# A list scheduler's model of its transfers: a later landing and a lower rate

## The chip, the cores and the metric

One core of one Trainium2 chip runs the kernel alone. The metric is device time in microseconds (us) for one execution. Engines are named as the profile names them: PE (matrix products; PEld loads its weights), DVE (vector), ACT (scalar), POOL (GpSimd) and SP (SyncE, which only issues DMAs here).

## The reference, cut to what matters

Two layers of a decoder trunk run for a prompt of 1024 tokens and for 8 samples of 4 tokens; both share the weights. Width is 1024, everything is float32.

```
layer 0:  h = rmsnorm(x);  proj = h @ w_in_a              # 3 groups x 4 heads x (q, k, v), and 4 cross queries
          mix = dilated sliding-window attention, 3 groups combined per head
                (prompt: banded softmax; samples: caches of 128, 512 and 2048 rows)
layer 1:  h = rmsnorm(x);  proj = h @ w_in_b
          mix = S5 state space (32 groups x 64 complex states), gelu, gated by w_glu
both:     cross = 4-head attention into 256 memory tokens (k, v = rmsnorm(mem) @ w_mem_kv)
          x = x + [mix | cross] @ w_out
          f = silu(a) * b  with  a, b = causal conv3(rmsnorm(x) @ w_up);   x = x + f @ w_down
outputs:  y of both, the updated caches, memory k/v, S5 states and conv states
```

## The kernel before

All 1056 tokens (1024 and 32) stand along the free dimension, in three column groups of 352, and 128 features on the partitions. A float32 product is made of three matmuls on a high and a low half (`mm3`); a weight tile is loaded by SP (`wload`, usually 512 KB), its high half is cast by ACT (`whigh`) and its low half is the difference, made by DVE or POOL (`wlow`). A pool of 20 buffers "B" holds raw and split weights and most activations.

The order of all instructions is written out when the program is built, by a list scheduler in the kernel itself. The dense products form a main stream; everything else (attention, sample attention, cross attention, S5, loading and turning inputs) consists of generators in 14 `Lane`s. After each `mm3` the main stream calls `pump`, which steps a lane when its gate is open. The gate (`gate`, `due`, `ready`) compares a clock that the scheduler keeps, `Meter`, with the time at which the operands of the lane's next step will be there by that clock. `Meter.note` books each instruction: a duration from the operation and size for the four computing engines, and for a DMA the issue, then a landing on a serial queue per issuing engine. `wtick` uses the same clock to decide when `whigh` and `wlow` are put out. Where nothing is left for the main stream, `until` calls `pump(True)`, which steps the lane with the earliest gate even if it isn't open. The engines then run their programs in order, with semaphores for the data: an instruction put out before its data is there blocks what is behind it on its engine.

`Meter` doesn't model the wait of a DMA for a free buffer. A step that is placed by its position in a loop, as the weight splits and reloads inside `up_tiles` and `hid_group` (the FFN), doesn't ask the clock.

Steps that the text below names: `x_turn`, `x_squares`, `x_norm` and `x_scale` load the input rows in nine tiles, transpose them on PE, take sums of squares on ACT, and make the normed halves in A tiles; `mem_kv` is the main stream beside them. `attn`, `scores` and `combine_head` are the prompt's attention, with partial results through DRAM (`og`, `xm`). `swa` is the samples' attention on DVE, with the caches in two 1 MB ring tiles in pool L, one fetched ahead, in lane 2, which `pump` serves last. `cross_s` is the samples' cross attention, whose memory rows POOL loads. In layer 1 `s5_u_evac` writes u to DRAM (`d_u`), reads it back in eight slices and appends `s5_states`, whose first step waits for them; `s5_out` uses `d_t` and `d_cl`.

Every operation passes through the wrapper at L216, so all rows have that line and are told apart by tile names.

Of the kernel before, what the change touches and what calls it, by code (L numbers as in the profile page):

```python
# [111 lines left out]
class Meter:  # L112
# [51 lines left out]
    def note(self, eng, op, args, kw):  # L164
        outs = [kw[k] for k in ("out", "accum_out") if kw.get(k) is not None] or [args[0]]
        ins = list(args["out" not in kw:]) + [v for k, v in kw.items() if k not in ("out", "accum_out")]
        ins = [a for a in ins if hasattr(a, "tensor")]
        out = outs[0]
        n = out.free_size()
        src = next((a for a in ins if a.free_size() >= n), out)  # L170
        start = max(self.t[eng], self.ready(ins, eng), *(self.used.get(o.tensor.name, 0.0) if o.space == bass.MemoryType.PSUM else 0.0 for o in outs))
        if op == "dma_start":
            if out.space != bass.MemoryType.DRAM:
                start = max(start, self.t["tensor"] - 4.0)
            self.t[eng] = start + (1.0 if eng == "gpsimd" else 0.05)
            self.dma[eng] = max(self.dma.get(eng, 0.0), self.t[eng] + 1.6) + n * out.ap[0][1] * 4 / 350e3
            end = self.dma[eng] + 0.2
        else:
            if eng == "tensor":
                wide = ins[0].dtype == F32  # L180
                turn = op == "transpose"
                cost = 0.107 if turn else max(n * 4 / 2400 + 0.008, 0.107) + 0.03 if wide else max(n / 2400, 0.025) + 0.0025
            elif eng == "scalar":
                vecs = sum(hasattr(kw.get(x), "tensor") for x in ("scale", "bias", "accum_out"))
                cost = (0.051 if src.space == bass.MemoryType.PSUM else 0.094) + n * 0.833e-3 + 0.0935 * vecs
            elif eng == "gpsimd":
                cost = 0.147 + n * 2.105e-3
            else:
                k = max(n, src.free_size()) if op.startswith("reduce") else n
                vecs = any(hasattr(kw.get(x), "tensor") for x in ("scalar", "scalar1", "scalar2"))  # L190
                fast = op == "tensor_scalar" and all(a.space != bass.MemoryType.PSUM for a in ins + outs)
                cost = 0.065 + 0.065 * vecs + k * 1.04e-3 * (6 if op == "reciprocal" else 0.5 if fast else 1)
            end = self.t[eng] = start + cost
        for o in outs:
            lo, hi = self.span(o)
            w = self.written.setdefault(o.tensor.name, [])
            w[:] = [x for x in w if not (lo <= x[0] and x[1] <= hi)] + [(lo, hi, end, eng if op != "dma_start" else "dma")]
        for a in ins + outs:
            self.used[a.tensor.name] = max(self.used.get(a.tensor.name, 0.0), end)
# [2409 lines left out]
```

## Time and profile before

| | us |
|---|---|
| median of 3 runs (2932.32 to 2938.57) | 2933.89 |
| the profiled execution | 2938.67 |
| its span, first to last instruction | 2936.7 |
| PE busy | 2735.2 (93%) |
| PEld busy | 2612.5 (89%) |
| DVE busy | 2070.4 (71%) |
| ACT busy | 1216.3 (41%) |
| POOL busy | 560.1 (19%) |

The mean granted PE clock is 0.972 of full speed. The DMA queues moved 431.56 MB, 147 GB/s over the span. PE is the engine that is nearly always busy, so a change of the time has to be a change of PE's idle time or of its clock; the other engines' idle time matters only where PE waits behind it.

### The profile page before, as it was taken

What the parts mean: (1) busy time and instruction counts of PE and PEld (TensorE: products, weight loads), DVE (VectorE), ACT (ScalarE), POOL (GpSimd) and SP (SyncE); (2) the same over time, 40 slices, a digit from 0 to 9 for tenths busy, and PEclk for the clock granted to TensorE, in tenths of its full rate; (3) what the DMA queues carried; (4) which work ended last, traced back from release to release, by engine and by line L of the source; (5) the groups of instructions that cost most, each with busy time, mean ns of one, the idle gap of its engine ahead of it and who ended that gap; (6) DMA issues with size and microseconds to landing.
All of it is one profiled execution on the core that took longest, in us unless ns stands there. A gap on an engine that the chain in (4) does not pass through costs nothing.

```text
span 2936.7 us, 50915 instructions
## 1 busy us (share of the span) xinstructions
PE 2735.2 (93%) x18896; PEld 2612.5 (89%) x18896; DVE 2070.4 (71%) x5937; ACT 1216.3 (41%) x3045; POOL 560.1 (19%) x551
## 2 busy tenths in 40 slices
PE   6999889999979999999998997888999999999999
PEld 5899778999969989999998887777998999999998
DVE  7477776787895777878859876645468787886434
ACT  6455554454542544444421123245344444443211
POOL 3221222322334400000022344011250000001220
PEclk8999999999989999999999998999999999999999
DMA  7234765666583423333482524843443234336421
GB/s 246 82 86 129 210 192 175 171 185 195 172 226 129 155 87 116 123 116 123 143 270 83 186 84 163 242 132 99 166 147 123 95 123 131 109 131 230 148 95 60
DMA packets 378883, 431.56 MB, mean 147 GB/s; under 512 B 31190, under 2 KB 333300, under 8 KB 377212
## 3 DMA queue, kind: packets, MB, share of 16 engines
q1 hardware_dynamic: 335516, 364.23, 38.9%
q0 software_dynamic: 20048, 47.95, 5.7%
q10 hardware_dynamic: 23072, 16.14, 2.0%
q8 instruction: 149, 2.44, 0.3%
q14 instruction: 98, 0.80, 0.1%
HBM read 345.10 MB, written 172.37 MB: 176 GB/s over the span
## 4 chain that ended last, share of the span: by engine, by line
PE 43%; DVE 37%; ACT 11%; issue 4%; DMA 4%; ACTq 1%; POOL 1%; SPq 0%; DVEq 0%; POOLq 0%
PE pd L216 34%; DVE B L216 21%; PE pm L216 9%; ACT B L216 7%; DVE S L216 6%; DVE T L216 3%; DVE L L216 3%; DVE M L216 3%; ACT S L216 2%; DMA L<-in_cache_win_kv 1%; ACT M L216 1%; ACT A L216 1%; DVE A L216 1%; ACTq L216 1%; ACT L L216 1%
## 5 line engine op out<-in xcount | busy, mean ns | idle before, releaser
L216 PE MATMUL pd<-A,B 128*128 128x352 f32 (+2 forms) x10992 | 1790.4, 317 | 44.1 <-DVE B L216 32.6
L216 PEld LDWEIGHTS pd<-A,B 128*128 128x128 f32 x10992 | 1645.9, 190 | 74.7 <-issue 39.4
L216 ACT CAST B<-B 128x512 fp32r<-128x512 f32 (+4 forms) x430 | 313.8, 751 | 618.1 <-DVE B L216 320.9
L216 POOL TENSOR_TENSOR B<-B,B 128x1024 fp32r<-128x1024 f32 (+3 forms) x95 | 236.9, 2494 | 1703.7 <-ACT B L216 1410.8
L216 DVE TENSOR_TENSOR B<-B,B 128x512 fp32r<-128x512 f32 (+5 forms) x517 | 409.5, 800 | 212.5 <-ACT B L216 205.6
L216 PE MATMUL pd<-L,B 128*128 128x264 f32 (+1 forms) x2976 | 449.7, 303 | 18.6 <-DVE L L216 9.5
L216 PEld LDWEIGHTS pd<-L,B 128*128 128x128 f32 x2976 | 417.0, 190 | 22.6 <-DVE L L216 10.2
L216 DVE TENSOR_TENSOR B<-pd,B 128x352 f32<-128x352 f32 x408 | 202.4, 518 | 222.0 <-PE pd L216 221.0
L216 ACT COPY B<-pm 128x512 f32<-128x512 f32 (+5 forms) x261 | 129.9, 507 | 211.2 <-PE pm L216 198.5
L216 PE MATMUL pd<-B,B 128*128 128x264 f32 (+2 forms) x1308 | 201.9, 303 | 2.5 <-POOL B L216 2.0
L216 DVE SCALAR_TENSOR_TENSOR B<-B,S,B 128x1023 f32<-128x1023 f32 (+1 forms) x152 | 198.3, 1305 | 0.0
L216 PE MATMUL pm<-const,B 128*128 128x128 f32 (+6 forms) x1103 | 161.4, 276 | 35.6 <-DVE B L216 7.8
L216 PEld LDWEIGHTS pd<-B,B 128*128 128x128 f32 x1308 | 179.6, 188 | 6.7 <-POOL B L216 2.6
L216 PEld LDWEIGHTS pm<-const,B 128*128 128x128 f32 (+4 forms) x1103 | 130.0, 148 | 56.9 <-issue 17.4
L216 ACT COPY S<-pm 128x256 f32<-128x256 f32 (+5 forms) x281 | 89.6, 346 | 166.2 <-PE pm L216 157.5
L216 ACT CAST A<-B 128x352 fp32r<-128x352 f32 (+3 forms) x148 | 97.5, 669 | 141.3 <-DVE B L216 49.9
L216 ACT COPY B<-pd 128x352 f32<-128x352 f32 (+4 forms) x211 | 103.6, 540 | 98.9 <-PE pd L216 90.3
L216 PE MATMUL pm<-const,S 128*128 128x128 f32 (+3 forms) x468 | 86.5, 292 | 45.5 <-DVE S L216 23.3
L216 DVE SCALAR_TENSOR_TENSOR L<-L,T,L 128x128 f32<-128x128 f32 x404 | 121.0, 375 | 3.7 <-DMA L<-in_cache_win_kv 3.6
L216 ACT ACTIVATE B<-B 128x352 f32<-128x352 f32 (+3 forms) x127 | 94.6, 750 | 68.7 <-DVE B L216 64.9
L216 PEld LDWEIGHTS pm<-const,S 128*128 128x128 f32 (+2 forms) x468 | 60.3, 159 | 65.0 <-ACT S L216 24.8
L216 DVE TENSOR_TENSOR A<-B,A 128x1056 fp32r<-128x1056 f32 (+3 forms) x78 | 92.5, 1193 | 11.8 <-ACT A L216 11.5
(210 smaller groups left out, 2628.9 us busy)
## 6 DMA issues: line engine op xcount, KB each, us to landing
B<-in_w_up SPq DMA_DIRECT2D x88, 512.0 KB
hd<-B SPq DMA_DIRECT2D x44, 528.0 KB
B<-hd SPq DMA_DIRECT2D x44, 528.0 KB
B<-in_w_down SPq DMA_DIRECT2D x44, 512.0 KB
B<-in_w_in_a SPq DMA_DIRECT2D x40, 512.0 KB
B<-xsp SPq DMA_DIRECT2D x32, 528.0 KB
L<-in_cache_win_kv SPq DMA_DIRECT2D x16, 1024.0 KB
L<-in_cache_win_kv SPq DMA_DIRECT2D x64, 256.0 KB
```

Source lines behind the costliest of these rows:

```text
L216: return f(*args, **kw)
```

## The change

In the booking of a DMA, the time between its issue and the earliest begin of its bytes goes from 1.6 to 2.2 us, and the rate of the queue from 350 to 250 bytes a nanosecond. No instruction, size or buffer is changed by itself; the order in which the generators are interleaved may change wherever a gate hangs on a DMA.

```diff
             self.t[eng] = start + (1.0 if eng == "gpsimd" else 0.05)
-            self.dma[eng] = max(self.dma.get(eng, 0.0), self.t[eng] + 1.6) + n * out.ap[0][1] * 4 / 350e3
+            self.dma[eng] = max(self.dma.get(eng, 0.0), self.t[eng] + 2.2) + n * out.ap[0][1] * 4 / 250e3
             end = self.dma[eng] + 0.2
```

Here `n * out.ap[0][1] * 4` is the size in bytes, `start` the time at which the issuing engine is free and the source is written, and `end` the landing that `ready` returns (0.2 us more is added for another engine's use of it).

## Rows read from the trace of the kernel before

**Rows 1.** Busy time by stretch: length, PE, PEld, DVE, ACT, POOL, granted clock, DMA.

```profile
0.00:80.00 80.00, 55.86 (x285) 46.86 (x285) 60.41 (x139) 48.61 (x93) 30.24 (x29) 0.87 0.74 244
80.00:800.00 720.00, 667.84 (x4438) 631.93 (x4439) 519.75 (x2532) 371.15 (x1212) 177.90 (x197) 0.97 0.55 157
800.00:900.00 100.00, 82.47 (x447) 73.15 (x446) 88.50 (x330) 41.78 (x114) 33.83 (x29) 0.90 0.78 227
...
1040.00:1470.00 430.00, 413.41 (x3302) 409.02 (x3301) 347.14 (x613) 195.09 (x443) 4.67 (x2) 0.99 0.38 123
1470.00:1690.00 220.00, 205.55 (x1279) 197.15 (x1278) 173.21 (x562) 43.81 (x61) 61.37 (x54) 0.98 0.53 177
1690.00:2060.00 370.00, 319.62 (x2098) 283.10 (x2099) 224.72 (x564) 146.12 (x369) 86.28 (x106) 0.94 0.48 144
...
2660.00:2937.00 277.00, 269.13 (x1711) 266.49 (x1709) 122.83 (x191) 56.74 (x72) 45.42 (x18) 0.99 0.38 133
```

**Rows 2.** Waits of PE over the span: us in total, times, longest us.

```profile
PE pd L216 <- DVE B L216: 43.2, 51, 5.4
PE pm L216 <- ACT S L216: 32.5, 30, 4.7
PE pm L216 <- DVE S L216: 23.3, 17, 9.2
...
PE pm L216 <- DMA B<-in_g_mix: 7.3, 1, 7.3
...
PE pm L216 <- DMA L<-d_u: 4.7, 2, 3.0
...
PE pm L216 <- DMA B<-d_cl: 0.9, 1, 0.9
```

**Rows 3.** Waits of DVE and ACT for DMAs, the same columns.

```profile
ACT A L216 <- DMA B<-hd: 39.8, 8, 17.7
ACT B L216 <- DMA B<-in_w_down: 38.8, 8, 9.7
...
DVE T L216 <- DMA B<-og: 11.5, 5, 5.5
...
DVE M L216 <- DMA L<-scr: 4.2, 2, 2.7
...
DVE L L216 <- DMA L<-in_cache_win_kv: 3.6, 2, 2.5
...
DVE M L216 <- DMA L<-in_cache_win_kv: 3.2, 3, 2.8
```

**Rows 4.** DMA issues of POOL: count, KB each, median us from issue to landing.

```profile
L<-scr POOLq DMA_DIRECT2D x36, 256.0 KB, 4.6
...
B<-in_cache_mem_kv POOLq DMA_DIRECT2D x16, 512.0 KB, 6.1
...
A<-in_cache_mem_kv POOLq DMA_DIRECT2D x16, 512.0 KB, 4.3
...
d_t<-M POOLq DMA_DIRECT2D x1, 2048.0 KB, 12.9
...
d_win<-S POOLq DMA_DIRECT2D x16, 128.0 KB, 2.0
```

**Rows 5.** Timeline of SP around the first read of d_u: start, length, what.

```profile
1824.45 0.63 SPq L216 DMA_DIRECT2D d_u<-B  x1
...
1829.01 5.36 SPq L216 DMA_DIRECT2D L<-d_u  x8
```

**Rows 6.** Timeline of PE there, with the idle time before a row.

```profile
1836.75 0.69 PE L216 MATMUL pm<-L,B 128*64 128x136 f32 x8 [3.01 <-DMA L<-d_u]
...
1886.94 0.69 PE L216 MATMUL pm<-L,B 128*64 128x136 f32 x8 [1.74 <-DMA L<-d_u]
```

**Rows 7.** Timeline of PE in the first stretch.

```profile
34.25 0.49 PE L216 MATMUL pm<-const,B 96*128 96x96 f32 x4
...
46.88 1.60 PE L216 MATMUL pd<-M,const 128*128 128x128 f32 x6 [2.75 <-DVE M L216]
49.64 1.59 PE L216 MATMUL pd<-M,const 128*128 128x128 f32 x6 [1.16 <-DVE M L216]
...
63.20 0.66 PE L216 MATMUL pd<-A,B 128*128 128x352 f32 x1 [9.18 <-ACT A L216]
```

**Rows 8.** Timeline of ACT in the first stretch: the last row's sum of squares.

```profile
43.06 1.06 ACT L216 ACTIVATE B<-B 96x1024 f32<-96x1024 f32 x1
```

**Rows 9.** Groups of DVE in 800:900: count, busy us, mean ns.

```profile
L216 DVE SCALAR_TENSOR_TENSOR L<-L,T,L 128x128 f32<-128x128 f32 x68 | 18.7, 347 | 0.0
```

## The prediction, made before the change was run

> **What bounds the kernel now.** The busy table by stretch comes first [rows 1]. PE is busy in nearly all of each stretch; what is left over is PE's idle time: 24.1 us in 0:80 (80 less 55.86), 52.2 in 80:800, 17.5 in 800:900, 16.6 in 1040:1470, 14.5 in 1470:1690, 50.4 in 1690:2060, 7.9 in 2660:2937. The whole span has 201.5 us of it (2936.7 less 2735.2). An edit that adds no work and removes none can move the time only inside these 201.5 us, and through the clock where PE pauses (0.87 in 0:80, 0.90 in 800:900). The second view is the waits of PE [rows 2]: most of them are for DVE and ACT results; only 12.9 us are direct waits for a DMA (7.3 + 4.7 + 0.9), and the 7.3 is the first transfer of all, which no order changes. The third is the waits of DVE and ACT for DMAs [rows 3]: these say where a consumer was put out before its data had landed, which is what the edited lines are about. The fourth is how long a transfer really takes [rows 4], as far as the trace has it (POOL's issues; for SP's there is no landing column, so SP's are read from a wait that a landing ended).
>
> **The change part by part.** It removes and adds no instruction. It moves consumers of DMAs later in the order, by what the booked landing grows: 0.6 us a transfer, and bytes/250 less bytes/350 a nanosecond. For 512 KB (524,288 bytes) that is 1.50 us of bytes before and 2.10 after. Booked from issue to landing: SP 0.05 + 1.6 + 1.50 + 0.2 = 3.35 before, 4.55 after; POOL, with 1.0 for the issue, 4.30 and 5.50. The trace has 4.3 and 6.1 us for POOL's 512 KB, 4.6 for 256 KB (booked 3.55, then 4.45), 12.9 for 2 MB (8.8, then 11.8) and 2.0 for 128 KB (3.2, then 3.9) [rows 4]. So the new booking is nearer for large and crowded transfers and further off for small ones.
>
> The Trainium skill (DMA: Bandwidth & Descriptors, section Anatomy of one DMA — SWDGE (gpsimd) path) gives about 2.0 us plus bytes at 436 GB/s for a DMA of this path. By that page 512 KB would estimate at 3.2 us, the old booking would be late enough already, and the change would only delay; the trace's 6.1 and 4.6 disagree with it, its 2.0 for 128 KB agrees.
>
> *Beginning, 0:80.* No engine waited for an input tile: the only wait for a DMA there is that for g_mix [rows 2], so later bookings can only hold consumers back. The queue carries 2 memory tiles, 9 input tiles and 8 weight tiles before the last input tile is due: some 19 times 0.6 us of bytes, 11.4 us; the clock of the main stream itself starts about 2 us later, because its first operands are booked later too, and three of the tiles are smaller. I take the last tile's turn as 6.5 us later against the main stream. In the trace that turn is at 34.25 [rows 7], but ACT takes its sum of squares only at 43.06 [rows 8], 8 us after the turn ended: ACT is behind, and this backlog hides the delay as long as ACT has other work. What is late next is the chain that PE already waits for: 2.75 + 1.16 + 9.18 us for the normed input [rows 7]. Bounds: nothing (all in ACT's backlog) and +7 (none of it). I take the middle, +3.5, because ACT's other work there, the weight casts, can't all move forward.
>
> *S5's read-back, 1690:2060.* The first slice chain is booked as: write of 512 KB and 64 KB, two tables of 512 KB, eight reads of 72 KB, all serial: before, 1.65 + 1.50 + 0.19 + 3.00 + 8 x 0.21 + 0.2 = 8.2 us; after, 2.25 + 2.10 + 0.26 + 4.19 + 8 x 0.29 + 0.2 = 11.4 us. In the trace the write is issued at 1824.45 [rows 5] and PE is released by the last read at 1836.75 [rows 6], 12.3 us. The 3.2 us later booking therefore covers the 3.01 us that PE stood, and the 1.74 us of the second such place; dense matmuls of the main stream take their place, and the lane's data come no later than before. Bounds: -5.6 (4.7 + 0.9, all direct waits but the first) and 0 (a lane step blocked a little later by something else). I take -4.5, nearest to the row.
>
> *Combining the heads, mostly 80:800.* DVE stood 11.5 us in 5 waits for og [rows 3]. Three loads of 260 KB in a row are booked 1.65 + 3 x 0.76 + 0.2 = 4.1, after it 2.25 + 3 x 1.07 + 0.2 = 5.7: up to 1.5 us of each wait goes, 7.5 us of DVE time. DVE is busy 519.75 of 720 us there [rows 1], so most of it was no loss to PE. Bounds -7.5 and 0; taken -2.
>
> *Samples' cross attention, 1690:2060.* Its ring loads landed in 4.3 us and were booked at 4.30; they will be booked at 5.50, 1.2 us too late. Two lanes take four rounds of two loads: 4 x 2 x 1.2 = 9.6 us at most, but the next round is fetched while one is worked on, which hides it; without that cover the lanes end up to 5 us later, in a stretch where PE is idle for 50.4 us anyway. Bounds 0 and +5; taken +1.
>
> *FFN, 1040:1470, 2265:2660 and the down projections.* ACT's largest waits for DMAs are here, 39.8 and 38.8 us [rows 3]. But the loads and splits stand at fixed places, and PE is busy 269.13 of 277 us with them in 2660:2937 [rows 1]. Taken 0, bounds -2 and +2.
>
> *Everything else.* Each gate that opens later lets another lane go first, and that shifts all that follows in 80:900 and 1690:2060. Of the 120.1 us of PE idle time there (52.2 + 17.5 + 50.4) a tenth either way is 12 us. I take 0, and keep both ends.
>
> Sum: +3.5 - 4.5 - 2 + 1 = -2.0 us. The profiled execution took 2938.67, 1.97 more than its span and 4.78 more than the median of the runs shown. 2938.67 - 2.0 = 2936.7 for such an execution; in terms of the median, 2933.89 - 2.0 = 2932 us.
>
> **The rivals.** *The sample attention falls behind (slower).* A ring tile of `swa` comes as one 1 MB load or four of 256 KB; four are booked 0.05 + 1.6 + 4 x 0.75 + 0.2 = 4.8 us before, 6.6 after. One is fetched ahead, and one tile's work is 16 operations of 347 ns [rows 9], 5.6 us: before, the booked landing was just inside the work that covers it, after it is just outside. Then each tile waits some 1 us by the scheduler's clock, the lane that is served last loses its turn, and its last tiles are pushed to 800:900, where DVE is already busy 88.5 of 100 us. Two tiles late cost 11 to 12 us of DVE there, which PE waits for: -2 + 12 = +10, 2944 us. It decides from the point where the lane enters 800:900 with two tiles more than now. For it: the chain there is DVE's. Against: DVE's own bookings, not the landings, may set the lane's pace, since DVE waited for these tiles only 3.6 + 3.2 us.
>
> *Stalls go everywhere (faster).* If an order with truer landings spares PE an eighth of its waits for ACT S, DVE S and DVE B (32.5 + 23.3 + 43.2 = 99 us) [rows 2], that is 12 us more: -14, 2920 us. For it: blocks on DVE and ACT are what PE waits for. Against: only 23 us of DVE's waits are for DMAs at all.
>
> *Nothing hangs on it.* Gates set by engines and free PSUM banks instead of landings leave the order as it is: 2934 us. Against it: og and d_u were early by the rows.
>
> *Landings were right already.* If 512 KB mostly lands about when it was booked before, as in POOL's 4.3 us for the cross attention's ring [rows 4], the late bookings hold back the beginning and the cross attention, +3.5 + 1, and spare nothing: 2938 us. Against it: 6.1 us for the same size in the other ring, and the 12.3 us of the read-back. The page of the Trainium skill named above, DMA: Bandwidth & Descriptors, speaks for it.
>
> **How the numbers follow.** Forecast 0.40, with its own range 2924 to 2940; sample attention late 0.22; stalls go 0.24; nothing 0.07; landings right 0.07. About 0.2% (5.9 us, below 2928 or above 2940) is what a measurement of this kernel can tell. Faster: 0.23 of the faster rival and 0.08 of the forecast, 0.31. Slower: 0.21 of the slower rival and 0.05 of the forecast and of the last, 0.26. Same: 0.43. The range goes from a little under the faster rival, 2917, to some way over the slower one, 2949.
>
> **What would show it.** Right: the waits of PE for d_u and d_cl are gone, those of DVE for og are near 4 us, PE's idle time in 0:80 is 3 to 4 us more, and the FFN stretches keep their lengths within 2 us. Wrong: 0:80 is no longer or is 8 us longer; the d_u waits stay; 800:900's work takes 10 us more with DVE full (sample attention); or the difference stands in 80:800, spread over many waits for ACT and DVE, which no term of the sum has.

## The result, and the profile after

The changed kernel takes 2966.38 us (median of 4 runs, 2964.05 to 2973.09), the kernel before 2936.23 in the runs beside it: a ratio of 1.0110, 95% interval 1.0090 to 1.0129. It is slower by 30 us, outside the predicted range. The page of the profiled execution (2973.09 us) has the busy times, and the granted clock in 40 slices:

```profile
span 2971.2 us, 50957 instructions
...
PE 2753.0 (93%) x18896; PEld 2622.7 (88%) x18896; DVE 2072.2 (70%) x5940; ACT 1217.5 (41%) x3045; POOL 547.5 (18%) x548
...
PEclk8999999999989999999999998989999999999999
```

PE has the same 18,896 instructions as before. In this pair of profiles it is busy 17.8 us longer for them (2753.0 less 2735.2) and idle 16.7 us longer (218.2 less 201.5), and the mean granted clock is 0.967 in place of 0.972: for the same products a lower clock shows as a longer busy time. How large this part of the loss is can't be read from one pair. The profiled execution is the longest of the four and has the lowest clock (the other three: 0.968, 0.970 and 0.971), and the profile of `st_rest` below is 18.9 us longer than before with PE busy only 3.6 us longer. The waits of PE over the span, against [rows 2]:

```profile
PE pd L216 <- DVE B L216: 54.5, 63, 3.3
PE pm L216 <- ACT S L216: 46.9, 28, 13.0
PE pm L216 <- DVE S L216: 19.9, 16, 9.0
...
PE pm L216 <- DMA B<-in_g_mix: 7.2, 1, 7.2
```

The waits for d_u and d_cl [rows 2] are gone, as predicted. The waits for ACT S grew from 32.5 to 46.9 us, the longest from 4.7 to 13.0, and DVE B (the low halves of weights are written there) from 51 waits to 63. Against [rows 3], DVE and ACT:

```profile
ACT A L216 <- DMA B<-hd: 38.3, 10, 12.5
ACT B L216 <- DMA B<-in_w_down: 31.4, 6, 13.1
...
ACT L L216 <- DMA d_y<-L: 23.7, 2, 18.9
```

```profile
DVE T L216 <- DMA B<-og: 1.8, 1, 1.8
```

DVE's wait for og fell from 11.5 to 1.8 us. ACT's longest stand for `d_y<-L`, which is a store of its own, grew from 10.7 us, once, to 18.9. The kernel before has this row for it:

```profile
ACT L L216 <- DMA d_y<-L: 10.7, 1, 10.7
```

Against [rows 4], this page also has landings of SP's DMAs (count, KB each, median us from issue to landing):

```profile
B<-in_w_up SPq DMA_DIRECT2D x88, 512.0 KB, 5.2
...
B<-in_w_down SPq DMA_DIRECT2D x44, 512.0 KB, 4.6
...
L<-in_cache_win_kv SPq DMA_DIRECT2D x64, 256.0 KB, 5.3
```

The 512 KB weight tiles of the feed-forward blocks land on SP after 4.6 to 5.2 us, where 3.35 was booked before and 4.55 now. So for these the new numbers are nearer, and the kernel is slower with them. No one pair of numbers fits all: SP's other 512 KB transfers have medians from 2.6 us (`out_y_prompt`) to 10.9 (`B<-d_win`) on the same page.

To see where, the dense matmuls of the main stream are counted. There are 15,360 of them, in the same order in every kernel here, so a block of time is what lies between two of them. How much longer each block is than before, in us, from one profile each (the blocks are named by the times of before; the last column is the whole span):

```
                    0-68  68-969  969-1457  1457-1729  1729-2093  2093-2666  2666-2928 |  span
changed             +3.8   +11.2      +0.0       +8.9       +6.4       +0.8       +3.3 | +34.4
lat_only            +2.0    +0.4      +0.6       +4.6       -6.2       +4.1       -0.3 |  +5.3
rate_only           +1.1    -4.9      +1.0       +5.6       +4.3       +1.5       +3.4 | +12.1
earlier             +5.1    +7.7      -0.4       -1.6      +17.6       +1.4       -0.3 | +30.1
tiny                +3.4    +2.5      +0.1       -0.7       -0.2       +1.9       -0.0 |  +7.0
st_begin            +3.6    +0.7      -0.2       +0.0       +1.9       -0.0       +0.0 |  +6.1
st_att              +2.0   +11.3      +0.0       +1.0       +4.1       +2.6       +0.0 | +21.0
st_rest             +2.4    -6.0      -0.2       +8.8       +9.9       +0.9       +3.1 | +18.9
after_dy_pool       +3.7    +8.0      +1.3       +7.9       -8.7       -0.0       +3.3 | +16.0
before_dy_pool      +1.1    -3.3      -0.2       +0.5       -4.6       +0.1       -0.2 |  -6.1
s5_new_dy_pool      +0.2    -3.4      -0.0       +0.8      -12.4       +0.8       +0.3 | -13.6
s5_new_dy_pool_gate +0.2    -0.1      +0.2       +1.2       -9.4       +1.4       -0.1 |  -6.2
swa_old             +3.8    +6.6      +0.8       +5.2       -2.9       +1.8       +3.2 | +18.4
swa_new             +4.0    +0.1      -0.0       +2.9       +2.2       +0.0       -0.1 |  +9.2
ffn0_new            +4.7    -1.3      -0.4      +12.0       +0.7       -0.2       -0.3 | +15.3
st_att_gate         +2.0   +21.9      +1.5       +2.2       +1.2       -2.9       +0.0 | +25.9
before_gate         +1.8    +4.6      -0.4       -0.5       +2.6       -0.2       -0.1 |  +7.9
```

How far one profile can be trusted is read from four kernels whose booking is that of before up to 969 (st_rest, before_dy_pool, s5_new_dy_pool, ffn0_new): 0-68 comes out +0.2 to +4.7 there, 68-969 -6.0 to -1.3. The +3.8 of the beginning is therefore no finding; the +11.2, and the +8.9 and +3.3 further on (within 3 and 0.3 us of before wherever the booking there was the old one), are. In 1729-2093, kernels with the old booking and the old S5 stores come out +0.7 to +4.1 (st_begin, st_att, swa_new, ffn0_new, st_att_gate, before_gate), so the changed kernel's +6.4 alone would say little; what S5 costs is read from the tests on it below.

### The profile page after: what moved, and what is told of

Same layout as the page of the kernel before. It is cut to its first block, busy times and chain, and to the rows that moved or that the text cites. A ratio compares the mean times of both kernels' runs of the same rounds, so it can differ in the third digit from the quotient of the medians.

```text
span 2971.2 us, 50957 instructions
## 1 busy us (share of the span) xinstructions
PE 2753.0 (93%) x18896; PEld 2622.7 (88%) x18896; DVE 2072.2 (70%) x5940; ACT 1217.5 (41%) x3045; POOL 547.5 (18%) x548
## 5 line engine op out<-in xcount | busy, mean ns | idle before, releaser
L216 DVE TENSOR_TENSOR B<-B,B 128x512 fp32r<-128x512 f32 (+5 forms) x524 | 417.1, 805 | 218.4 <-ACT B L216 210.3
L216 POOL TENSOR_TENSOR B<-B,B 128x1024 fp32r<-128x1024 f32 (+3 forms) x88 | 218.0, 2479 | 1726.7 <-ACT B L216 1479.8
L216 PE MATMUL pd<-B,B 128*128 128x264 f32 (+4 forms) x1322 | 211.0, 307 | 13.5 <-DVE B L216 10.6
L216 ACT COPY B<-pm 128x512 f32<-128x512 f32 (+3 forms) x260 | 129.8, 511 | 214.9 <-PE pm L216 206.8
L216 PE MATMUL pm<-const,B 128*128 128x128 f32 (+5 forms) x1111 | 162.0, 276 | 34.9 <-issue 14.6
L216 ACT COPY S<-pm 128x256 f32<-128x256 f32 (+4 forms) x278 | 89.0, 347 | 175.5 <-PE pm L216 167.4
L216 DVE CUSTOM_DVE_ANT_0 M<-L,L 128x128 f32<-128x128 f32 x384 | 94.9, 311 | 13.7 <-PE pm L216 3.8
```

Source lines behind the costliest of these rows:

```text
L216: return f(*args, **kw)
```

## The experiments

Times are medians; each ratio is against the kernel before, run beside it.

**Which of the two numbers, and which direction.** Four versions of the booked line: only the later landing (2.2 us, 350), only the lower rate (1.6 us, 250), the opposite of the change, and a tiny change.

```diff
-self.t[eng] + 1.6) + n * out.ap[0][1] * 4 / 350e3    # before
+self.t[eng] + 1.0) + n * out.ap[0][1] * 4 / 583e3    # earlier
+self.t[eng] + 1.65) + n * out.ap[0][1] * 4 / 345e3   # tiny
```

lat_only: 

> Only the begin of the bytes is booked later (2.2 us), the rate stays 350. Theory 1 (later bookings hold lanes back, in proportion): between before and after, about +12 to +20 us of the +30. Theory 2 (any other order of the lanes costs, whatever the booking says): some +10 to +35 us, no relation to the size of the edit. Rival (only the sample attention's 1 MB tiles matter, by their bytes): within 8 us of before.

rate_only: 

> Only the rate is booked lower (250), the begin stays at 1.6 us. Theory 1: +10 to +20 us. Theory 2: +10 to +35 us with its losses in other places than those of the full change. Rival (sample attention by its bytes): nearly the whole +30, with 18 us of it between 725 and 985.

earlier: 

> The opposite edit of the same size: begin 1.0 us, 583 bytes a nanosecond. Theory 1: no slower than before, the first 80 us some 0 to 4 us shorter, the read-back of d_u stands longer (+2 to +5). Theory 2: slower by 10 us or more, too, though the edit has the other sign.

tiny: 

> A very small edit of the same sign: 1.65 us and 345 bytes a nanosecond; a 512 KB transfer is booked 0.07 us later. Theory 1: within 3 us of before. Theory 2: it moves the time by several us in either direction, as its order differs in all queues.

Measured: lat_only 2943.81, ratio 1.0010 (0.9995 to 1.0024); rate_only 2950.62, 1.0029 (1.0017 to 1.0040); earlier 2969.16, 1.0096 (1.0071 to 1.0122); tiny 2945.67, 1.0015 (0.9997 to 1.0034). The halves come to 0.4% and the whole to 1.1%, so they don't add up, and both halves lie below what either theory had expected of them. Booking *earlier* costs as much as booking later, so a theory that later bookings cost in proportion to how much later they are is out. But it costs in another way. In `earlier` PE itself waits for transfers:

```profile
PE pm L216 <- DMA L<-d_u: 13.1, 2, 7.1
PE pm L216 <- DMA B<-in_state_s: 11.7, 1, 11.7
```

Both waits lie in its longest block, 1729-2093 (+17.6). The kernel before waits 4.7 us for d_u [rows 2] and never for `in_state_s` (a little ahead of that place it stands 9.2 us for DVE S, which `earlier` doesn't, so not all of the 11.7 is new); the changed kernel waits for neither. So consumers put out too soon cost here what the booking is meant to prevent, and the loss of the changed kernel is of another kind.

**Which part of the program.** The new numbers hold only in one part (`self.lat, self.rate` in the booked line, set in `run`): up to the first `mem_kv`, from there to the end of the first output projection, or from the first feed-forward block on.

```diff
         kmt, kv = self.mem_kv(0)
+        self.m.lat, self.m.rate = 2.2, 250e3      # st_att: from here ...
...
+        self.m.lat, self.m.rate = 1.6, 350e3      # ... to here
         self.bulk_on = True
         self.drain(0)
         self.ffn(0, self.s5_prep())
```

st_begin: 

> The new booking holds only up to the end of the first layer's memory keys and values (the first 70 us or so); behind that the old one. Theory A, the stages add up: the time is 3 to 4 us above the kernel before (the beginning was 3.8 us longer in the changed kernel's trace), and the stretches from 68 us on keep their lengths within 2 us each. Theory B, what comes behind depends on every start: the beginning is 3 to 4 us longer and some later stretch differs by more than 5 us in either direction.

st_att: 

> The new booking holds only from the attention on to the end of the first layer's output projection (about 70 to 1040 us). Theory A, the stages add up: 729 to 969 us is about 18 us longer as in the changed kernel, 438 to 729 some 10 us shorter, the whole 8 to 14 us above before, and 1040 us onward keeps its lengths. Theory B: the attention comes out otherwise, since its lanes start at another place of the main stream than in the changed kernel; any of -5 to +20.

st_rest: 

> The new booking holds only from the first feed-forward block on (about 1040 us). Theory A, the stages add up: the first 1040 us keep their length within 1 us, 1457 to 1729 is 9 us longer, 1729 to 1855 7 us shorter, 1855 to 2093 13 us longer, the whole 15 to 20 us above before. Theory B: as the order in front is that of before, the later stretches are as in the kernel before or differ with no relation to the changed kernel's.

Measured: st_begin 2943.90, 1.0010 (0.9997 to 1.0023); st_att 2952.76, 1.0044 (1.0027 to 1.0062); st_rest 2960.44, 1.0066 (1.0040 to 1.0093). Here the excesses do add up, 1.2% against 1.1%, and block by block the table repeats the changed kernel's (68-969 in st_att; 1457-1729 and 2666-2928 in st_rest; least well 1729-2093, +9.9 against +6.4). So what is lost in one part depends little on the part in front, and the parts can be looked at one by one.

**S5: ACT stands at a DMA issue.** The trace of the changed kernel, ACT, then SP, then PE around PE's longest wait (start, length, what, and in brackets the idle time before it):

```profile
1889.33 1.17 ACT L216 ACTIVATE L<-L 128x1152 f32<-128x1152 f32 x1
1901.38 7.97 ACTq L216 DMA_DIRECT2D d_y<-L  x8
1909.38 0.37 ACT L216 COPY L<-pm 128x256 f32<-128x256 f32 x1 [18.88 <-DMA d_y<-L]
```

```profile
1896.22 4.43 SPq L216 DMA_DIRECT2D L<-d_u  x8
```

```profile
1896.10 0.74 PE L216 MATMUL pd<-A,B 128*128 128x352 f32 x3
1909.88 4.50 PE L216 MATMUL pm<-L,B 128*128 128x144 f32 x24 [13.04 <-ACT S L216]
...
1914.90 2.72 PE L216 MATMUL pm<-L,B 128*128 128x144 f32 x24
```

ACT's gelu ends at 1890.50. Its eight stores of y come next in its program, need nothing else by their data, and are issued only from 1901.38 on; behind them stand the evictions that PE waits for. The semaphore event that let ACT go at 1901.3 belongs to the landing of SP's reads of d_u, put out at 1896.22. In the trace every DMA of SP and of ACT reports its landing to one of the same eight semaphores (108 to 115), and POOL's report to eight others (99 to 106). The first store waits for 114, on which the third of the d_u reads lands at 1901.3. The eighth is issued at 1909.03 and waits for 113, on which a cache copy of SP lands at 1909.01. So a store whose semaphore a transfer of SP still holds waits for that transfer, though it needs none of its data. Semaphores of their own for ACT's stores weren't tried. The clock follows (columns: stretch, length, PE, PEld, DVE, ACT, POOL, clock, DMA):

```profile
1880.00:1900.00 20.00, 16.24 (x127) 12.45 (x126) 11.26 (x17) 5.01 (x14) 0.00 (x0) 1.00 0.90 257
1900.00:1920.00 20.00, 10.12 (x66) 8.61 (x67) 8.98 (x15) 4.08 (x13) 0.00 (x0) 0.66 0.71 225
```

The stretch with PE's pause is granted 0.66 where the one ahead had 1.00, and PE pays for the pause again when it goes on: the 24 products behind it take 4.50 us, the next 24 of the same shape 2.72. That is 1.8 us more. In 1729-2093 as a whole PE is busy only 1.2 us longer than before, so this pause is not where the 17.8 us of busy time come from; by the profiles they lie in 0-68 (+4.2), 68-969 (+6.3) and 1457-1729 (+6.0). The Trainium skill (Perfetto Trace Analysis, section DMA Instruction — HWDGE (DVE, Sync)) says that on trn2 the DMA engines don't wait on semaphores, and its diagram puts the wait on the issuing engine's sequencer; the 10.9 us between ACT's gelu and its first store (1890.50 to 1901.38) agree. The test: the stores are issued by POOL.

```diff
-            nc.scalar.dma_start(out=yv[tau][:, m * 8:m * 8 + 8, :], in_=y[tau * 16:(tau + 1) * 16])
+            nc.gpsimd.dma_start(out=yv[tau][:, m * 8:m * 8 + 8, :], in_=y[tau * 16:(tau + 1) * 16])
```

after_dy_pool (on the changed kernel): 

> The changed kernel, with the eight stores of each S5 output slice issued by POOL in place of ACT. Theory A, ACT stands at the issue of these stores until a transfer of SP's queue has landed: PE's wait of 13.04 us for ACT near 1909 us is gone, 1855 to 2001 us is 8 to 14 us shorter than in the changed kernel, the whole 2952 to 2960 us. Theory B, the order alone costs it (the evictions are late in ACT's row, with or without the issue): PE waits as long there for ACT, and the time stays within 4 us of the changed kernel's 2966. POOL's own issues (about 1 us each, 64 of them) could be late for others: then new waits for d_y and over 2970 us.

before_dy_pool (on the kernel before): 

> The kernel before, with S5's output stores issued by POOL, booking unchanged. Before, ACT's largest wait at these issues cost PE 3 us. Theory A: 0 to 4 us below before, so that the gain of the version with the new booking in S5 is mostly the booking's. Theory B, moving the stores changes the order enough to matter by itself: more than 5 us either way.

Measured: after_dy_pool 2948.17, 1.0029 (1.0013 to 1.0045); before_dy_pool 2931.51, 0.9971 (0.9960 to 0.9983). ACT in after_dy_pool, then POOL, and the waits of PE from 1853 to 2106 us:

```profile
1889.39 1.17 ACT L216 ACTIVATE L<-L 128x1152 f32<-128x1152 f32 x1
1892.38 0.38 ACT L216 COPY L<-pm 128x256 f32<-128x256 f32 x1 [1.82 <-PE pm L216]
```

```profile
1890.85 4.24 POOL L216 DMA_DIRECT2D d_y<-L  x8 [48.17 <-ACT L L216]
```

```profile
PE pm L216 <- ACT S L216: 10.1, 6, 2.9
```

POOL issues the stores at once, ACT goes on after 1.82 us and then waits only for PE, and PE's longest wait for ACT S there is 2.9 us. The same edit takes 18 us off the changed kernel (2966.38 less 2948.17, more than expected) and 8.5 off the one before. So some 10 us, a third of the change's loss, go with the stores standing on ACT longer than before. The two kernels were measured beside different runs of the kernel before: by the ratios it is 0.81% less 0.29%, some 15 us, and by the profiles of 1729-2093 it is 10.5. That the edit was worth 8.5 us without the change had not been expected to that size (0 to 4 us): in the trace of before, ACT already stood 10.7 us for such a store, once.

**The feed-forward blocks.** In ffn0_new the new numbers hold only in the call `self.ffn(0, self.s5_prep())`.

ffn0_new: 

> The new booking holds only in the first feed-forward block and the S5 preparation beside it (about 1040 to 1700 us). If that block's own bookings cost the 9 us of 1457 to 1729: that stretch is 7 to 9 us longer, PE waits for DVE's weight splits 12 to 14 times in place of 9, and the time is 5 to 12 us above before, unless S5 behind it gives it back. If the 9 us are work that only moved there from S5: that stretch is longer, 1729 to 2093 is as much shorter, and the time is within 4 us of before.

Measured: 2952.64, ratio 1.0046 (1.0030 to 1.0061). 1457-1729 is 12.0 us longer, PE waits for DVE's weight splits there 13 times in place of 8, and 1729-2093 gives nothing back (+0.7). The block loses time by its own bookings. PE of the changed kernel in the down projections of both blocks, DVE in the first, and then PE of ffn0_new:

```profile
1506.85 0.91 PE L216 MATMUL pd<-B,B 128*128 128x352 f32 x4 [1.43 <-DVE B L216]
...
1520.16 0.92 PE L216 MATMUL pd<-B,B 128*128 128x352 f32 x4 [1.43 <-DVE B L216]
...
2718.61 0.91 PE L216 MATMUL pd<-B,B 128*128 128x352 f32 x4 [1.43 <-DVE B L216]
...
2731.89 0.91 PE L216 MATMUL pd<-B,B 128*128 128x352 f32 x4 [1.42 <-DVE B L216]
```

```profile
1505.14 0.53 DVE L216 TENSOR_TENSOR B<-pd,B 128x352 f32<-128x352 f32 x1 [1.42 <-PE pd L216]
1505.58 1.22 DVE L216 TENSOR_TENSOR B<-B,B 128x1024 fp32r<-128x1024 f32 x1
```

```profile
1494.99 0.91 PE L216 MATMUL pd<-B,B 128*128 128x352 f32 x4 [1.43 <-DVE B L216]
...
1508.34 0.91 PE L216 MATMUL pd<-B,B 128*128 128x352 f32 x4 [1.43 <-DVE B L216]
```

The DVE row at 1505.58 is the low half of a w_down tile. It stands behind the eviction of the products ahead (1505.14), and PE starts the tile's own products as it ends. In the kernel before these waits don't exist; the halves of these two tiles are ready 3 and 7 us ahead of their use (at 1490.1 and 1501.7 by the count of matmuls), one made by DVE, one by POOL:

```profile
1485.81 1.22 DVE L216 TENSOR_TENSOR B<-B,B 128x1024 fp32r<-128x1024 f32 x1
```

```profile
1492.73 2.41 POOL L216 TENSOR_TENSOR B<-B,B 128x1024 fp32r<-128x1024 f32 x1 [21.45 <-ACT B L216]
```

Two places in the code make a low half: `wtick`, ahead of the use, once the raw tile has landed by the scheduler's clock, and `wneed`, at the use. With the landing booked later these tiles fell to `wneed`. Two such places make 2666-2928 3.3 us longer, and are 3.6 us of 1457-1729 (120 matmuls take 21.1 us in place of 19.3, twice). Of the other 5 us there, 1 is eight small products of the S5 preparation that lay behind 1729 before. The rest lies beside that preparation, where DVE is nearly full (116 of 125 us in 1540:1665 of the kernel before), and wasn't taken apart.

**The attention: two causes that fell.** First the predicted slow rival, the ring of `swa`: its loads alone are booked in the old way on the changed kernel, and alone in the new way on the kernel before.

```diff
         def fetch(s, ci):
             t = self.ring[self.nring % 2]
             self.nring += 1
+            self.m.lat, self.m.rate = 1.6, 350e3     # swa_old; 2.2, 250e3 in swa_new
...
+            self.m.lat, self.m.rate = 2.2, 250e3     # swa_old; 1.6, 350e3 in swa_new
             return v
```

swa_old: 

> The changed kernel, with the samples' sliding attention's own ring loads booked as before (1.6 us, 350 bytes a nanosecond), all other transfers as changed. If the ring's booked landing, now just outside the work that covers it, lets this lane fall behind: it ends near main-stream matmul 3230 again in place of 3291, the 18 us of 729 to 969 go, and the time is 2945 to 2952. If the lane falls behind for another reason: it ends after matmul 3270 and 729 to 969 stays 10 to 20 us longer than before.

swa_new: 

> The kernel before, with only the ring loads of the samples' sliding attention booked in the new way. If these bookings are what holds that lane back: 729 to 969 is 10 to 18 us longer and the time 2945 to 2955. If not: 729 to 969 within 5 us of before, the whole within 6 us.

Measured: swa_old 2968.66, 1.0090 (1.0068 to 1.0113); swa_new 2944.18, 1.0017 (1.0003 to 1.0031). The lane's last DVE operation comes at main-stream matmul 3228 before and 3291 in the changed kernel; it comes at 3221 in swa_old and at 3277 in swa_new. So the ring's own bookings do hold the lane back, as the rival said. With it work moves across 729: in swa_new 68 to 729 is 12.1 us shorter and 729 to 969, as expected, 12.3 longer. In the changed kernel the two are 7.0 shorter and 18.2 longer, in swa_old 4.1 shorter and 10.6 longer. The lateness itself is therefore nearly free: swa_new pays 4 us, and swa_old, with the lane in time, stays as slow as the changed kernel. Then a single stand that the trace offers. Of st_att, ACT and PE:

```profile
807.45 0.54 ACT L216 ACTIVATE T<-T 128x4 f32<-128x4 f32 x2 [6.45 <-DVE T L216]
```

```profile
810.71 1.12 PE L216 MATMUL pm<-const,B 128*128 128x128 f32 x4 [5.65 <-DVE A L216]
```

The samples' exponential stood in ACT's program ahead of the memory tiles' casts before DVE had made its input; PE waited for what was behind it. The test gives the exponentials gates of their own, in st_att and in the kernel before:

```diff
+                    yield ACT, al
                     nc.scalar.activation(out=al, in_=al, func=AF.Exp, scale=SCALE)
...
+                yield ACT, sf
                 nc.scalar.activation(out=sf, in_=sf, func=AF.Exp, scale=SCALE)
```

st_att_gate: 

> The new booking holds only from the attention to the first output projection (as in the run that cost 0.44%), and the samples' attention puts its two exponentials out under gates of their own, once the scheduler's clock has ACT and their input ready. If ACT's stand of 6.45 us for this exponential in front of the memory tiles' casts is what costs the attention's time: PE's wait of 5.65 us near 811 us is gone, 729 to 969 is 6 to 12 us shorter than without the gates, and the time is 2938 to 2946. If the loss is spread over the order: another wait of that size appears, and the time stays within 4 us of 2952.

before_gate: 

> The kernel before with the same two gates, booking unchanged. There ACT stood only 0.58 us for that exponential, so by the theory of the stand the gates are worth nothing here: within 4 us of before. If the gates help or hurt by themselves through the order they make: more than 5 us either way, and the run above says less.

Measured: st_att_gate 2963.93, 1.0083 (1.0064 to 1.0103); before_gate 2943.98, 1.0014 (1.0004 to 1.0024). The 6.45 us stand is gone, another took its place, and the version is 11 us slower than st_att. PE in st_att_gate:

```profile
838.24 1.22 PE L216 MATMUL pd<-B,A 128*128 128x512 f32 x2 [7.57 <-DVE B L216]
```

729 to 969 is 24.4 us longer than before, where st_att has 17.8. So taking the largest wait away didn't win its time back. The gates also change the order by themselves: before_gate is 0.14% slower, with 68 to 729 13.3 us longer and 729 to 969 8.8 shorter. What makes up the 13 us of the attention, and which bookings bring them about, stays open.

**A version that beats both.** The new numbers only from S5's start to the second feed-forward block, where the read-back needs them, and the y stores on POOL; then with the gates as well.

s5_new_dy_pool: 

> The new booking holds only from the start of S5 to before the second feed-forward block (about 1730 to 2660 us), and S5's output stores are issued by POOL. Theory A, the stages add up and ACT's standing at its store issues was the price of S5: 1457 to 1729 keeps its length (the 9 us were those of the first feed-forward block's own bookings), 1729 to 1855 is 7 us shorter, 1855 to 2093 about 2 us shorter, so 4 to 9 us below before. Theory B: with another order in the feed-forward block in front, S5 comes out otherwise; then within 4 us of before or above it.

s5_new_dy_pool_gate: 

> The version with the new booking in S5 alone and S5's stores on POOL (0.44% below before), with the two gates as well. If the gates are worth nothing where ACT didn't stand: 2924 to 2931. If they disturb the order in front of S5: 2932 or more; if they also help: below 2922.

Measured: s5_new_dy_pool 2927.34, ratio 0.9956 (0.9940 to 0.9972), 13 us below the kernel before, more than expected, and 39 below the changed one; with the gates 2932.56, 0.9979 (0.9967 to 0.9991), some 5 us slower than without, though these intervals overlap. Against before_dy_pool the booking itself gives 4.2 us (2931.51 less 2927.34; the intervals overlap), and 1729-2093 is 7.8 us shorter by the profiles.

## Why the prediction was wrong, point by point

- *FFN, "Taken 0, bounds -2 and +2".* This step failed by its reason. That "the loads and splits stand at fixed places" holds for `up_tiles` and `hid_group`, but the w_down tiles are split by `wtick`, which asks the booked landing. The two blocks are 8.9 us (1457-1729) and 3.3 (2666-2928) longer; ffn0_new shows the first alone at 13.5 us by the medians. The late splits are shown for 3.6 and 3.3 us of it, the rest of the first is open.
- *"Everything else", "I take 0" with 12 us either way.* This step failed by its size and by its shape: it was one term where two large ones lay, and both were losses. The attention took 11.2 us (st_att alone: 13.5 by the medians), and S5's stores some 10, with PE's wait of 13.04 us as the largest. Why the attention lost is open. The bound, a tenth of PE's idle time, was a guess that no row supports, and it had no term for the clock, though the prediction had named the clock as the second way to lose time: in the profiled pair PE is busy 10.5 us longer ahead of 969.
- *S5's read-back, -4.5.* Right for the waits it was about: those for d_u and d_cl are gone, and with the stores off ACT the booking is worth 4.2 us, though the intervals overlap. The gain didn't show in the changed kernel, whose 1729-2093 is 6.4 us longer. The step had "dense matmuls of the main stream take their place"; what came as well was ACT at its store issue, which the prediction didn't look at though ACT already stood there in the trace of before.
- *Combining the heads, -2.* The mechanism was right, og's waits fell from 11.5 to 1.8 us. What it gave PE can't be told apart within the attention's loss.
- *Beginning, +3.5.* Not settled. st_begin's +4.7 us has an interval that takes in zero, and kernels with the old order there scatter as far.
- *Cross attention, +1.* Not tried by itself.
- *The rivals.* The sample attention did fall behind by 63 main-stream matmuls; its ring alone puts it 49 behind, at a price near 4 us and not 12. The sign given for this rival did come, in part: the matmuls of 800:900 take 12.6 us longer in the changed kernel (798.6 to 911.2), but DVE is no fuller there (81.84 us busy in 800:900, 88.50 before). "Stalls go everywhere" went the other way: the waits for ACT S, DVE S and DVE B grew from 99 to 121 us. "Nothing hangs on it" is out. "Landings were right already" is refuted by 4.6 to 5.2 us for SP's 512 KB weight tiles. By the page named in the prediction, the Trainium skill's DMA: Bandwidth & Descriptors, the estimate was 3.2 us; POOL's 512 KB take 4.4 and 6.0 us in the changed kernel, so the measurement decides against it. Yet the kernel did become slower, as that rival had it, by far more than its 4 us.

## What to carry to other kernels

In this list scheduler a more truthful number was no improvement by itself: of the 16 variants 13 were slower by the median (three of them with an interval that takes in no change), in either direction of the edit, and the three that were faster all had a stand removed, by POOL's stores. Two things are worth trying first elsewhere: to change the booking only where a wait for that transfer is seen, and to search for engines that stand at a DMA issue, since everything behind it in that engine's program stood too. And before costing a step at nothing because its place in the program is fixed, find every reader of the changed number: here `wtick` was one.

## What was not expected of the hardware

A store issued by ACT waited 10.9 us (1890.50 to 1901.38) for no data of its own, released by the landing of another queue's transfer on a semaphore that the two share. PE lost 13.04 us, and its next 24 products took 4.50 us in place of 2.72, in a stretch with a granted clock of 0.66. POOL's issues of the same stores began 0.3 us after the data (1890.85 against a gelu that ended at 1890.56).
